# The squares of a norm added up on VectorE, with one ones-matmul for each norm instead of eight

## The chip, the cores and the metric

The kernel runs on one core of a Trainium2 chip. Five engines work side by side and signal each other by semaphores: TensorE (PE, matrix products from SBUF into PSUM banks), VectorE (DVE), ScalarE (ACT), GpSimd (POOL) and SyncE (SP), which issues the loads of weights. The metric is the time of one launch on the device in microseconds (us).

## The reference, cut to what matters

The program computes two model parts one after the other on 256 tokens of 1024 numbers, in float32. The first part has two layers; 16 meta tokens stand ahead of the sequence, so it works on 272 tokens:

```python
def rmsnorm(x, g):
    y = x32 * lax.rsqrt(jnp.mean(x32 * x32, axis=-1, keepdims=True) + NORM_EPS)
    return (y * g.astype(jnp.float32)).astype(x.dtype)

for l in range(DEPTH):                                   # DEPTH = 2
    hn = rmsnorm(h, norm1_g[l])
    proj = hn @ w_in[l]                                  # q, k, v and the convolution's input
    ...                                                  # rotary embedding
    attn_out = diff_attention(q, k, v, lam, subln_g[l], lam_init)
    conv_out = conformer_conv(u + b_glu[l], ...)         # gated, causal, layer norm, swish
    h = h + jnp.concatenate([attn_out, conv_out], axis=-1) @ w_out[l]
    hn = rmsnorm(h, norm2_g[l])
    gate, up = jnp.split(hn @ w_gate_up[l], 2, axis=-1)
    h = h + (jax.nn.silu(gate) * up) @ w_down[l]
h = rmsnorm(h, final_g)
```

The second part normalises the result again (its gain is g_mix), scales and shifts it by numbers that a small matrix w_ada yields, runs a gated delta rule and a dilated attention on it (the mixer), and then a mixture of 64 experts with eight chosen for a token.

A norm needs one number for each token: the mean over 1024 channels of the squares. That is a sum across the partitions of SBUF and over eight tiles, and it is what the change is about.

## The kernel before, in words

Activations lie transposed: 128 channels on the partitions, tokens along a row, eight tiles (KC = 8) for the 1024 channels; h[:, k] is tile k, 272 (T) or 256 (S) columns wide. In layer 1 everything after the attention is computed for the 256 real tokens only.

**Weights and products.** `weights` loads a block of 1024 x 256 weights by SP into `raw`, casts it on ACT into `hi` (f32r, a float32 form that PE reads at its fast rate; two halves, L165) and computes the rest `lo` on DVE (L166, two halves). There are three slots each for raw, hi and lo; a cast into a slot waits until PE has finished with the block that was in it. `mm3` does each product in three f32r matmuls: hi by xh (L172), hi by xl (L173), lo by xh (L174), where xh + xl is the activation. `block2` takes two PSUM banks and runs all eight k for both. The pool `mm` has three PSUM banks: with gate banks pg[0] and pg[1] and the first up bank pu[0] taken, pu[1] waits for one of them to be evicted.

**The norm.** `norm_in` (L262 to L280) does not normalise its input. It casts h times the gain into xh (L270, ACT) and xl (L271, DVE), and the products run on these. Beside them it squares each tile on ACT (L275) and multiplies it by a matrix of ones on PE (L276, plain float32), eight times into one bank of the pool `ax`, so that every partition holds the sum of squares of each token. `rsqrt` then takes the square root on ACT (L201, out of the bank, with a table load ahead of it) and the reciprocal on DVE (L202): rstd. Only the evictions of the products multiply by rstd: L361 and L362 for w_in (the a and gate halves of the convolution's input), L589 and L590 for the gate and up halves of the FFN. So an mm bank can't be emptied before rstd is there.

`norm_in` is called four times: norm 1 of layer 0, norm 2 of layer 0, norm 1 of layer 1 (272 columns each) and norm 2 of layer 1 (256 columns). While the last FFN's w_down runs, `mix_tile` does the same for the two norms that meet there, the final one and the mixer's: per tile two squares (L662, one with final_g as its scale) and two ones-matmuls (L663), into two `ax` banks that `mix_begin` takes. `mixer` reads the first in L692 (m), the second in L695, and computes from them the factor with which the tiles hh and hl are made (L704, L705), which the mixer's first matmuls read.

**The order of the work.** Nothing is ordered by hand here. The program is written in sequence, and a scheduler with a simulated timeline decides the order of the instructions on each engine when the kernel is built; `high_priority(offset=...)` lets marked pieces move ahead (250 for weights and mix_tile, 200 for the squares, the ones-matmuls and rsqrt of a norm). On the chip each engine works through its list in that order. An instruction that is priced or placed differently can so change the order of others near it. At the end of layer 1's attention the scheduler interleaves the attention's last norm (L465 squares of the head outputs, L201 and L202 on `oss`, L468, L470, the transposes L474 on PE, and L477 and L478, which write the attention half of w_out's input `bigb`) with the convolution's channel norm (L512 to L515, L201 and L202 on `sd`, L519, the tanh L521, L522, L524, L526, L527, which write the other half).

Of the kernel before, what the change touches and what calls it, by code (L numbers as in the profile page):

```python
# [9 lines left out]
F32 = mybir.dt.float32  # L10
# [3 lines left out]
OP = mybir.AluOpType  # L14

NM, S, D = 16, 256, 1024
T = NM + S
QT = ((0, 16), (16, 128), (144, 128))
KC = D // 128
# [90 lines left out]
class K:  # L110
# [151 lines left out]
    def norm_in(s, h, g, t0, n):  # L262

        ap, A, V = s.ap, s.A, s.V
        xh = ap.tile([128, KC, T], F32R, name="xh")
        xl = ap.tile([128, KC, T], F32R, name="xl")
        ss = s.ax()
        sl = slice(t0, t0 + n)
        for k in range(KC):
            A.activation(xh[:, k, sl], h[:, k, sl], AF.Copy, scale=g[:, k:k + 1])  # L270
            V.scalar_tensor_tensor(xl[:, k, sl], h[:, k, sl], g[:, k:k + 1], xh[:, k, sl].bitcast(F32),  # L271
                                   op0=OP.mult, op1=OP.subtract)
            sq = ap.tile([128, T], F32, name="sq", bufs=3)
            with s.tc.high_priority(offset=200):
                A.activation(sq[:, :n], h[:, k, sl], AF.Square)  # L275
                s.PE.matmul(ss[:, :n], s.C["ones"], sq[:, :n], start=(k == 0), stop=(k == KC - 1))  # L276
        r = ap.tile([128, T], F32, name="rstd", bufs=2)
        with s.tc.high_priority(offset=200):
            s.rsqrt(r[:, sl], ss[:, :n], s.eps5, 1.0 / D)
        return (xh, xl), r  # L280

# [368 lines left out]
    def mix_begin(s):  # L650
        P, V, cp = s.P2, s.V, s.cp
        s.gm = cp.tile([128, KC], F32, name="gm")
        V.scalar_tensor_tensor(s.gm, s.mod[:, 1], 1.0, P["g_mix_2"], op0=OP.add, op1=OP.mult)
        V.tensor_tensor(s.gm, s.gm, P["final_g"], op=OP.mult)
        s.msum = (s.ax(), s.ax())

    def mix_tile(s, h, hg, k):

        A, PE, hs = s.A, s.PE, slice(NM, T)
        for p, g in zip(s.msum, (1.0, s.P2["final_g"][:, k:k + 1])):  # L660
            a = s.ap.tile([128, S], F32, name="nsq", **s.nsq)
            A.activation(a, h[:, k, hs], AF.Square, scale=g)  # L662
            PE.matmul(p[:, :S], s.C["ones"], a, start=(k == 0), stop=(k == KC - 1))  # L663
        A.activation(hg[:, k, hs], h[:, k, hs], AF.Copy, scale=s.gm[:, k:k + 1])

    def mixer(s):
# [1027 lines left out]
```

## Time and profile before

| | |
|---|---|
| median of 3 runs | 1671.23 us (1670.63 to 1674.64) |
| the profiled execution | 1669.04 us |
| its span, first to last instruction | 1667.2 us, mean granted clock 0.984 |
| busy: PE, DVE, ACT | 1598.1 us (96%), 865.5 us (52%), 744.5 us (45%) |
| PE MATMUL records of L276 and L663 | 64 and 32 |
| HBM, last 500 us | some 420 GB/s |

The span is that of the profiled execution, which is one run of its own; 1.8 us of its time lie outside the span. Busy shares of different engines overlap. The records of PE's matmuls overlap among themselves as well: each is longer than the distance to the next one's start, so time on PE is read from starts. The expert weights, 64 loads each of three matrices, are what moves in the last 500 us.

### The profile page before, as it was taken

The page shows a single profiled execution, that of the slowest core. Times are in us where ns is not written, and L with a number is a line of the kernel's source. Part 1 is how long each engine was busy: PE and PEld are TensorE (multiplying, and loading weights), DVE is VectorE, ACT ScalarE, POOL GpSimd, SP SyncE. Part 2 cuts the span into 40 slices and gives each one's busy share as a digit, 9 for nine tenths or more (in the row PEclk, how much of TensorE's full clock was granted, in tenths as well). Part 3 has the DMA queues.
Part 4 walks back from the last instruction along what each step waited for, and adds up shares of the span by engine and source line. Part 5 has one row for each costly group of instructions (what it writes and reads, how often), then busy time and mean ns, then how long its engine had stood idle before and what let it go on. Part 6 is the DMA issues. An engine that isn't in the chain of part 4 may idle for free.

```text
span 1667.2 us, 32866 instructions
## 1 busy us (share of the span) xinstructions
PE 1598.1 (96%) x13630; PEld 1358.0 (81%) x13630; DVE 865.5 (52%) x1764; ACT 744.5 (45%) x1492; POOL 14.4 (1%) x28
## 2 busy tenths in 40 slices
PE   7999999999999999989999999999899999999897
PEld 6966999999968999988999999999666576566463
DVE  6685766646987666458656654553422221222122
ACT  5376644445347544455856856643322211112121
POOL 2000000000000000000000000000000000000000
PEclk9999999999999999999999999999899999999999
DMA  8408655555466555754343342666799999999995
GB/s 249 140 26 274 194 179 174 172 172 174 130 203 192 176 189 171 234 167 140 114 128 102 102 129 89 233 191 223 285 365 421 420 419 420 420 420 420 420 420 243
DMA packets 209959, 389.29 MB, mean 234 GB/s; under 512 B 8855, under 2 KB 183313, under 8 KB 184977
## 3 DMA queue, kind: packets, MB, share of 16 engines
q1 hardware_dynamic: 209104, 386.66, 64.0%
q8 instruction: 108, 1.77, 0.5%
q0 software_dynamic: 704, 0.51, 0.3%
q14 instruction: 43, 0.34, 0.1%
HBM read 386.10 MB, written 1.05 MB: 232 GB/s over the span
## 4 chain that ended last, share of the span: by engine, by line
PE 76%; DMA 14%; ACT 5%; DVE 4%; issue 1%; SPq 0%; DVEq 0%; ACTq 0%
PE mm L172 14%; PE mm L173 14%; PE mm L174 14%; PE pm L1508 6%; DMA we<-in_w_exp_up 6%; PE pm L1534 4%; DMA we<-in_w_exp_down 3%; DMA we<-in_w_exp_gate 2%; PE pm L1472 2%; PE dx L488 2%; PE mm L195 2%; PE mm L196 1%; PE mm L197 1%; ACT hi L165 1%; DMA raw<-in_w_out 1%; PE dx L630 1%
## 5 line engine op out<-in xcount | busy, mean ns | idle before, releaser
L166 DVE TENSOR_TENSOR lo<-raw,hi 128x1024 fp32r<-128x1024 f32 (+2 forms) x300 | 347.9, 1192 | 144.2 <-ACT hi L165 142.9
L165 ACT CAST hi<-raw 128x1024 fp32r<-128x1024 f32 (+2 forms) x300 | 292.7, 1024 | 271.0 <-PE mm L173 150.5
L172 PE MATMUL mm<-xh,hi 128*128 128x272 f32 (+1 forms) x1008 | 288.1, 288 | 0.0
L173 PE MATMUL mm<-xl,hi 128*128 128x272 f32 (+1 forms) x1008 | 287.8, 286 | 0.0
L174 PE MATMUL mm<-xh,lo 128*128 128x272 f32 (+1 forms) x1008 | 286.6, 286 | 0.0
L1508 PE MATMUL pm<-we,xT 128*32 128x256 f32 (+2 forms) x2048 | 195.9, 392 | 8.4 <-DMA we<-in_w_exp_up 5.8
L173 PEld LDWEIGHTS mm<-xl,hi 128*128 128x128 f32 x1008 | 189.7, 188 | 0.9
L174 PEld LDWEIGHTS mm<-xh,lo 128*128 128x128 f32 x1008 | 189.4, 188 | 0.5
L172 PEld LDWEIGHTS mm<-xh,hi 128*128 128x128 f32 x1008 | 188.5, 188 | 0.7
L1508 PEld LDWEIGHTS pm<-we,xT 128*32 128x32 f32 (+2 forms) x2048 | 122.2, 129 | 76.0 <-DMA we<-in_w_exp_up 7.9
L173 PE MATMUL mm<-bigb,hi 128*128 128x256 f32 (+1 forms) x512 | 148.3, 290 | 0.1
L172 PE MATMUL mm<-hh,hi 128*128 128x256 f32 x384 | 110.6, 291 | 7.2 <-ACT hh L704 4.2
L1534 PE MATMUL pm<-we,hT 128*32 128x512 f32 (+2 forms) x512 | 112.5, 605 | 0.1
L173 PE MATMUL mm<-hl,hi 128*128 128x256 f32 x384 | 109.5, 286 | 0.7 <-DVE hl L705 0.7
L174 PE MATMUL mm<-hh,lo 128*128 128x256 f32 x384 | 108.4, 285 | 0.0
L1519 DVE SCALAR_TENSOR_TENSOR hp<-sil,cs,pm 128x256 f32<-128x256 f32 x26 | 17.6, 676 | 168.5 <-ACT sil L1517 168.5
L174 PE MATMUL mm<-biga,lo 128*128 128x272 f32 (+1 forms) x352 | 101.4, 288 | 0.0
L172 PE MATMUL mm<-biga,hi 128*128 128x272 f32 (+1 forms) x352 | 100.6, 286 | 0.0
L173 PEld LDWEIGHTS mm<-bigb,hi 128*128 128x128 f32 x512 | 97.5, 191 | 0.8 <-DVE bigb L478 0.3
L1539 DVE TENSOR_TENSOR y<-pm,gt 128x512 f32<-128x512 f32 x52 | 35.9, 689 | 119.5 <-PE pm L1534 119.5
L1517 ACT ACTIVATE sil<-pm 128x256 f32<-128x256 f32 x26 | 10.0, 384 | 175.2 <-PE pm L1508 175.2
L195 PE MATMUL mm<-hi,hh 128*128 128x256 f32 x288 | 85.8, 298 | 2.0 <-DVE cacc L861 2.0
(541 smaller groups left out, 3089.7 us busy)
## 6 DMA issues: line engine op xcount, KB each, us to landing
we<-in_w_exp_gate SPq DMA_DIRECT2D x64, 1024.0 KB, 19.6
we<-in_w_exp_up SPq DMA_DIRECT2D x64, 1024.0 KB, 19.8
we<-in_w_exp_down SPq DMA_DIRECT2D x64, 1024.0 KB, 19.7
raw<-in_w_in SPq DMA_DIRECT2D x62, 1024.0 KB, 5.3
raw<-in_w_gate_up SPq DMA_DIRECT2D x44, 1024.0 KB, 5.1
raw<-in_w_ada SPq DMA_DIRECT2D x22, 1024.0 KB, 6.0
raw<-in_w_down SPq DMA_DIRECT2D x16, 1024.0 KB, 5.1
raw<-in_w_out SPq DMA_DIRECT2D x12, 1024.0 KB, 6.7
```

What stands on the lines that cost most here:

```text
L165: s.A.copy(hi[:, a:b], raw[:, a:b])
L166: s.V.tensor_tensor(lo[:, a:b], raw[:, a:b], hi[:, a:b].bitcast(F32), op=OP.subtract)
L172: s.PE.matmul(ps[:, :n], a, xh, start=start, stop=False)
L173: s.PE.matmul(ps[:, :n], a, xl, start=False, stop=False)
L174: s.PE.matmul(ps[:, :n], b, xh, start=False, stop=stop)
L195: s.PE.matmul(p[:, :256], xh, w[0][:, k], start=(k == 0), stop=False)
L488: PE.matmul(p[:, :nq], dg, z[:, c, tq + j:tq + j + nq], start=(j == 0), stop=(j == n - 1))
L1472: s.PE.matmul(p[:, 256 * kk:256 * kk + 256], s.ht[h][:, i, k + kk], oh[:, i], start=(i == 0 and h == 0), stop=(i == 1 and h == 1))
L1508: mm = PE.matmul(gu[sg, 256 * m:256 * m + 256], xT[:, k, o + sg.start:o + sg.stop], w[m][:, k], start=(k == 0), stop=(k == 7))
L1519: V.scalar_tensor_tensor(hp.rearrange("p k q -> p q k"), sil.rearrange("p (q k) -> p q k", k=2), cs, gu[:, 256:].rearrange("p (q k) -> p q ...
L1534: PE.matmul(py[sg], hT[:, k, sg], w[2][:, k, 512 * j:512 * j + 512], start=(k == 0), stop=(k == 1))
L1539: V.tensor_tensor(y, py, s.gt2[:, 512 * j:512 * j + 512], op=OP.mult)
```

## The change

In `norm_in` the square of tile 0 is written into a tile `sqsum`, and DVE adds the other seven squares to it (L278 of the changed file). After the loop one ones-matmul (L282) sums `sqsum` over the partitions into the `ax` bank, which is taken only then, and rsqrt follows as before. In `mix_tile` two tiles msq0 and msq1 collect the squares (L668), and at the last tile the two banks are taken and two ones-matmuls issued (L672). The pool tiles borrow the places of tiles that exist already (tags sd and vf). Counted in the code, 32 + 16 ones-matmuls become 4 + 2, and 28 + 14 additions come in.

```diff
--- before.py
+++ after.py
@@ -264,18 +264,22 @@
         ap, A, V = s.ap, s.A, s.V
         xh = ap.tile([128, KC, T], F32R, name="xh")
         xl = ap.tile([128, KC, T], F32R, name="xl")
-        ss = s.ax()
         sl = slice(t0, t0 + n)
+        tot = ap.tile([128, T], F32, name="sqsum", tag="sd")
         for k in range(KC):
             A.activation(xh[:, k, sl], h[:, k, sl], AF.Copy, scale=g[:, k:k + 1])
             V.scalar_tensor_tensor(xl[:, k, sl], h[:, k, sl], g[:, k:k + 1], xh[:, k, sl].bitcast(F32),
                                    op0=OP.mult, op1=OP.subtract)
-            sq = ap.tile([128, T], F32, name="sq", bufs=3)
+
+            sq = ap.tile([128, T], F32, name="sq", bufs=3) if k else tot
             with s.tc.high_priority(offset=200):
                 A.activation(sq[:, :n], h[:, k, sl], AF.Square)
-                s.PE.matmul(ss[:, :n], s.C["ones"], sq[:, :n], start=(k == 0), stop=(k == KC - 1))
+                if k:
+                    V.tensor_tensor(tot[:, :n], tot[:, :n], sq[:, :n], op=OP.add)
         r = ap.tile([128, T], F32, name="rstd", bufs=2)
         with s.tc.high_priority(offset=200):
+            ss = s.ax()
+            s.PE.matmul(ss[:, :n], s.C["ones"], tot[:, :n], start=True, stop=True)
             s.rsqrt(r[:, sl], ss[:, :n], s.eps5, 1.0 / D)
         return (xh, xl), r
 
@@ -652,15 +656,20 @@
         s.gm = cp.tile([128, KC], F32, name="gm")
         V.scalar_tensor_tensor(s.gm, s.mod[:, 1], 1.0, P["g_mix_2"], op0=OP.add, op1=OP.mult)
         V.tensor_tensor(s.gm, s.gm, P["final_g"], op=OP.mult)
-        s.msum = (s.ax(), s.ax())
+        s.msq = [s.ap.tile([128, S], F32, name=f"msq{i}", tag=("sd", "vf")[i], bufs=1 + i) for i in range(2)]
 
     def mix_tile(s, h, hg, k):
 
         A, PE, hs = s.A, s.PE, slice(NM, T)
-        for p, g in zip(s.msum, (1.0, s.P2["final_g"][:, k:k + 1])):
-            a = s.ap.tile([128, S], F32, name="nsq", **s.nsq)
+        for t, g in zip(s.msq, (1.0, s.P2["final_g"][:, k:k + 1])):
+            a = s.ap.tile([128, S], F32, name="nsq", **s.nsq) if k else t
             A.activation(a, h[:, k, hs], AF.Square, scale=g)
-            PE.matmul(p[:, :S], s.C["ones"], a, start=(k == 0), stop=(k == KC - 1))
+            if k:
+                s.V.tensor_tensor(t, t, a, op=OP.add)
+        if k == KC - 1:
+            s.msum = (s.ax(), s.ax())
+            for p, t in zip(s.msum, s.msq):
+                PE.matmul(p[:, :S], s.C["ones"], t, start=True, stop=True)
         A.activation(hg[:, k, hs], h[:, k, hs], AF.Copy, scale=s.gm[:, k:k + 1])
 
     def mixer(s):
```

Behind `norm_in` the lines of the changed file are 4 higher, behind `mix_tile` 9: L589 becomes L593, L361 L365, L477 L481, L521 L525.

The scheduler's order moves in three places. In the rows below the number behind a name tells one buffer from another; a wait names the engine whose signal the instruction stands for.

First, norm 2 of layer 0, on ACT. hi_2142 is the fourth weight block of the FFN, rstd the factor. Before:

```order
L165 CAST hi_2134<-raw_2132 128x1024
L275 ACTIVATE sq_1992<-h_1743 128x272 [waits DVE_49,Activation_49]
L270 ACTIVATE xh_1952<-h_1743,pc_norm2_g_747 128x272
L201 ACT_TABLE_LOAD
L201 ACTIVATE rstd_1995<-ax_1954,eps5_75 128x272 [waits PE_49]
L165 CAST hi_2142<-raw_2140 128x1024 [waits DMAHW6_49,PE_49]
L165 CAST hi_2142<-raw_2140 128x1024
```

and now:

```order
L270 ACTIVATE xh_1952<-h_1743,pc_norm2_g_747 128x272
L276 ACTIVATE sq_1990<-h_1743 128x272 [waits DVE_49,Activation_49]
L270 ACTIVATE xh_1952<-h_1743,pc_norm2_g_747 128x272
L165 CAST hi_2142<-raw_2140 128x1024 [waits DMAHW6_49,PE_49]
L165 CAST hi_2142<-raw_2140 128x1024
L201 ACT_TABLE_LOAD
L201 ACTIVATE rstd_1993<-ax_1994,eps5_75 128x272 [waits PE_49]
```

The cast of hi_2142, which waits for PE to release a slot, stands ahead of the table load and the square root; before it stood behind them. Norm 2 of layer 1 shows the same exchange.

At the same place on PE (mm_2016 and mm_2017 are the gate banks of the first block, mm_2066 and mm_2067 its up banks). Before:

```order
L173 MATMUL mm_2017<-xl_1953,hi_2002 128x272
L276 MATMUL ax_1954<-sq_1992,blob0_73 128x272 [waits Activation_49]
L174 MATMUL mm_2017<-xh_1952,lo_2003 128x272
L172 MATMUL mm_2016<-xh_1952,hi_2002 128x272
L173 MATMUL mm_2016<-xl_1953,hi_2002 128x272 [waits DVE_49]
L174 MATMUL mm_2016<-xh_1952,lo_2003 128x272
L172 MATMUL mm_2017<-xh_1952,hi_2002 128x272
L173 MATMUL mm_2017<-xl_1953,hi_2002 128x272
```

and now:

```order
L174 MATMUL mm_2016<-xh_1952,lo_2003 128x272
L173 MATMUL mm_2017<-xl_1953,hi_2002 128x272
L174 MATMUL mm_2017<-xh_1952,lo_2003 128x272
L173 MATMUL mm_2066<-xl_1953,hi_2010 128x272
L282 MATMUL ax_1994<-sqsum_1954,blob0_73 128x272 [waits DVE_49]
L174 MATMUL mm_2066<-xh_1952,lo_2011 128x272
L172 MATMUL mm_2067<-xh_1952,hi_2010 128x272 [waits DVE_49]
L173 MATMUL mm_2067<-xl_1953,hi_2010 128x272
L174 MATMUL mm_2067<-xh_1952,lo_2011 128x272
```

Before, the last ones-matmul stood 38 places ahead of the first matmul into mm_2067; now the only one stands two places ahead of it, behind the last matmul that reads the first block's hi and lo (mm_2017 of lo_2003).

Second, norm 1 of layer 1, on DVE, where a1 and g1 are evictions of the a and gate halves. Before:

```order
L271 SCALAR_TENSOR_TENSOR xl_4094<-h_3452,pc_norm1_g_92,xh_4093 128x272 [waits DVE_49,Activation_49] x2
L202 RECIPROCAL rstd_4136<-rstd_4136 128x272 [waits Activation_49]
L361 TENSOR_TENSOR a1_4258<-mm_4158,rstd_4136 128x272 [waits DVE_49,PE_49]
L361 TENSOR_TENSOR a1_4265<-mm_4159,rstd_4136 128x272 [waits PE_49]
L369 TENSOR_TENSOR biga_4139<-blob1_181,rstd_4136 128x272
L370 TENSOR_TENSOR biga_4139<-blob1_181,rstd_4136 128x272
```

and now:

```order
L278 TENSOR_TENSOR sqsum_4095<-sqsum_4095,sq_4131 128x272 [waits DVE_49]
L202 RECIPROCAL rstd_4134<-rstd_4134 128x272 [waits Activation_49]
L166 TENSOR_TENSOR lo_4283<-raw_4280,hi_4282 128x1024 [waits DMAHW0_49,PE_49,Activation_49]
L166 TENSOR_TENSOR lo_4283<-raw_4280,hi_4282 128x1024 [waits Activation_49]
L365 TENSOR_TENSOR a1_4258<-mm_4158,rstd_4134 128x272 [waits DVE_49]
L366 TENSOR_TENSOR g1_4259<-mm_4208,rstd_4134 128x272 [waits PE_49]
L365 TENSOR_TENSOR a1_4265<-mm_4159,rstd_4134 128x272
```

The two halves of lo_4283 have come between the reciprocal and the first eviction. On ACT the square root stays ahead of the cast here, and on PE the ones-matmul stands ten places ahead of the first matmul into mm_4209.

Third, the end of layer 1's attention, on ACT. Before:

```order
L465 ACTIVATE scr_5034,oss_5015<-mm_5014,st_4749 128x128 [waits Activation_49]
L201 ACTIVATE oss_5015<-oss_5015,eps5_75 128x4 [waits Activation_49]
L201 ACTIVATE sd_5372<-ax_5371,eps5_75 128x256 [waits PE_49]
L477 ACTIVATE bigb_4140<-mm_5041,subg_749 128x4x128 [waits PE_49]
L521 ACT_TABLE_LOAD
L521 ACTIVATE sq_5393<-biga_4139,hlb_751,hlg_750 128x256 [waits DVE_49]
L521 ACTIVATE sq_5400<-biga_4139,hlb_751,hlg_750 128x256 [waits DVE_49]
L522 ACTIVATE biga_4139<-biga_4139,pc_norm2_g_747 128x256 [waits Activation_49]
L521 ACTIVATE sq_5407<-biga_4139,hlb_751,hlg_750 128x256 [waits DVE_49]
```

and now:

```order
L469 ACTIVATE scr_5034,oss_5015<-mm_5014,st_4749 128x128 [waits Activation_49]
L201 ACTIVATE sd_5372<-ax_5371,eps5_75 128x256 [waits PE_49]
L201 ACTIVATE oss_5015<-oss_5015,eps5_75 128x4 [waits Activation_49]
L525 ACT_TABLE_LOAD
L525 ACTIVATE sq_5393<-biga_4139,hlb_751,hlg_750 128x256 [waits DVE_49]
L525 ACTIVATE sq_5400<-biga_4139,hlb_751,hlg_750 128x256 [waits DVE_49]
L526 ACTIVATE biga_4139<-biga_4139,pc_norm2_g_747 128x256 [waits Activation_49]
L525 ACTIVATE sq_5407<-biga_4139,hlb_751,hlg_750 128x256 [waits DVE_49]
L526 ACTIVATE biga_4139<-biga_4139,pc_norm2_g_747 128x256 [waits Activation_49] x2
L530 ACTIVATE bigb_4140<-biga_4139 128x256 [waits DVE_49]
L525 ACTIVATE sq_5414<-biga_4139,hlb_751,hlg_750 128x256
L481 ACTIVATE bigb_4140<-mm_5041,subg_749 128x4x128 [waits PE_49]
```

L477 (now L481), which writes the attention half of w_out's input, followed the square roots; now the table load and eight instructions of the channel norm stand between.

## Rows read from the trace of the kernel before

**Rows 1.** The page: the chain that ended last, by engine.
```profile
PE 76%; DMA 14%; ACT 5%; DVE 4%; issue 1%; SPq 0%; DVEq 0%; ACTq 0%
```

**Rows 2.** By line: the ones-matmuls (count, ns min/median/max, first and last start).
```profile
L276 PE MATMUL ax<-sq,blob x64: 377/391/661, 18.3 to 546.9; 128*128 128x272 f32 x48, 128*128 128x256 f32 x16
...
L663 PE MATMUL ax<-nsq,blob x32: 377/379/483, 687.8 to 740.8; 128*128 128x256 f32 x32
```

**Rows 3.** Timeline, PE, norm 2 of layer 0 (start us, us, instruction, idle before).
```profile
199.19 0.62 PE L276 MATMUL ax<-sq,blob 128*128 128x272 f32 x2
199.45 0.49 PE L174 MATMUL mm<-xh,lo 128*128 128x272 f32 x1
199.77 0.29 PE L172 MATMUL mm<-xh,hi 128*128 128x272 f32 x1
...
201.41 0.29 PE L173 MATMUL mm<-xl,hi 128*128 128x272 f32 x1
```

**Rows 4.** Timeline, PE, norm 2 of layer 1.
```profile
546.73 0.59 PE L276 MATMUL ax<-sq,blob 128*128 128x256 f32 x2
...
547.27 0.28 PE L174 MATMUL mm<-xh,lo 128*128 128x256 f32 x1
```

**Rows 5.** Timeline, PE, norm 1 of layer 0.
```profile
18.33 2.47 PE L276 MATMUL ax<-sq,blob 128*128 128x272 f32 x6
```

**Rows 6.** Timeline, PE, the end of the last FFN and the mixer's start.
```profile
737.86 1.81 PE L663 MATMUL ax<-nsq,blob 128*128 128x256 f32 x6 [0.42 <-ACT nsq L662]
...
740.53 0.68 PE L663 MATMUL ax<-nsq,blob 128*128 128x256 f32 x2
...
745.48 0.79 PE L172 MATMUL mm<-hh,hi 128*128 128x256 f32 x2 [4.18 <-ACT hh L704]
```

**Rows 7.** By line: an addition of two such tiles on DVE.
```profile
L592 DVE TENSOR_TENSOR a<-a,g x44: 415/428/442, 205.8 to 668.6; 128x272 f32<-128x272 f32 x22, 128x256 f32<-128x256 f32 x22
```

**Rows 8.** Timeline, ACT, norm 2 of layer 0.
```profile
199.85 0.49 ACT L201 ACTIVATE rstd<-ax,eps 128x272 f32<-128x272 f32 x1 [1.38 <-PE ax L276]
201.74 2.00 ACT L165 CAST hi<-raw 128x1024 fp32r<-128x1024 f32 x2 [1.40 <-PE mm L173]
```

**Rows 9.** Timeline, ACT, ahead of w_out in layer 1.
```profile
513.60 0.47 ACT L201 ACTIVATE sd<-ax,eps 128x256 f32<-128x256 f32 x1
515.37 0.69 ACT L477 ACTIVATE bigb<-mm,subg 128x512 fp32r<-128x512 f32 x1 [1.30 <-PE mm L474]
516.07 1.28 ACT L521 ACT_TABLE_LOAD   x1
...
520.65 0.59 ACT L521 ACTIVATE sq<-biga,hlb,hlg 128x256 f32<-128x256 f32 x1
```

**Rows 10.** Timeline, DVE, norm 2 of layer 0.
```profile
200.37 1.85 DVE L202 RECIPROCAL rstd<-rstd 128x272 f32<-128x272 f32 x1 [2.09 <-ACT rstd L201]
202.33 0.79 DVE L589 TENSOR_TENSOR g<-mm,rstd 128x272 f32<-128x272 f32 x2
203.03 2.35 DVE L166 TENSOR_TENSOR lo<-raw,hi 128x1024 fp32r<-128x1024 f32 x2
```

**Rows 11.** Timeline, PE, the first matmul of w_out in layer 1.
```profile
516.11 0.50 PE L172 MATMUL mm<-bigb,hi 128*128 128x256 f32 x2 [0.78 <-ACT bigb L477]
```

**Rows 12.** Timeline, DVE, ahead of w_out in layer 1.
```profile
513.93 0.69 DVE L470 TENSOR_TENSOR osb<-mm,oss 128x512 f32<-128x512 f32 x1
514.53 1.74 DVE L202 RECIPROCAL sd<-sd 128x256 f32<-128x256 f32 x1
...
516.76 1.42 DVE L519 TENSOR_TENSOR biga<-biga,sd 128x256 f32<-128x256 f32 x4
```

**Rows 13.** Timeline, ACT, the end of the last FFN.
```profile
740.15 0.46 ACT L692 ACTIVATE m<-ax,eps 128x256 f32<-128x256 f32 x1
```

**Rows 14.** Windows: busy us by engine, granted clock (PEclk), DMA share, GB/s.
```profile
510.00:520.00 10.00, 6.97 (x44) 5.43 (x44) 7.03 (x13) 8.53 (x23) 0.00 (x0) 1.00 0.61 202
...
743.80:750.60 6.80, 4.43 (x19) 4.14 (x20) 6.58 (x18) 3.79 (x10) 0.00 (x0) 0.50 0.26 71
```

## Prediction

> **What bounds the kernel now.** I read the chain of work that ended last first: TensorE (PE) carries 76% of it, and DMA 14%, the expert weights at the end [rows 1]. An instruction taken off PE's stream before the experts is therefore time won, and a wait put into it is time lost. Next came the lines of the ones-matmuls: 64 records of L276 and 32 of L663, two records to each f32 matmul in the code, so 32 and 16 matmuls [rows 2]. Then I read PE's timeline around them, because records of one engine overlap and their lengths can't be added.
>
> **What a ones-matmul costs.** At the second norm of layer 0 the pair starts at 199.19; one matmul stands behind it, and the next starts at 199.77: 0.58 us for the pair and one ordinary slot. Thirteen slots lie between 199.77 and 201.41, 0.126 us each [rows 3]. The pair takes 0.58 - 0.126 = 0.455 us of the stream. With 256 columns it is 546.73 to 547.27, 0.54 less a slot of 0.12, so 0.42 us [rows 4]. The lengths of the two records (0.391 each by [rows 2]) would give 0.78 us.
> The Trainium skill ("FP8 and Floating Point Precision", TensorE Precision Notes) says that true FP32 goes through the array in four passes. By that rule one such matmul is worth four slots, by estimate 4 x 0.126 = 0.50 us; the trace has 0.455, so starts and rule stand together against the summed records. By the records all 42 removed matmuls would be worth 32 us, by the starts 18.
>
> **What the change removes.** Four calls of norm_in and one series of mix_tile, in order of time:
> - A, norm 1 of layer 0: 8 matmuls become 1. Six records stand alone from 18.33 to 20.43 ahead of the first weight matmul [rows 5]: 2.1 us at most; the others, four net, 4 x 0.455 = 1.8.
> - B, norm 2 of layer 0, and C, norm 1 of layer 1: 7 x 0.455 = 3.2 us each.
> - D, norm 2 of layer 1 (256 columns): 7 x 0.42 = 2.9.
> - E, the two sums of mix_tile: 16 become 2. Four pairs (six records from 737.86, two at 740.53) run in PE's idle tail before the mixer and save nothing [rows 6]; 12 x 0.42 = 5.0.
> All of it: 3.9 + 3.2 + 3.2 + 2.9 + 5.0 = 18.2 us.
>
> **What it adds.** 28 + 14 additions on VectorE (DVE), 0.43 us each by the like operation L592 [rows 7]: 18 us, on an engine that the page shows busy for 52% of the span. That alone would be covered. What counts is where the sum becomes ready. Before, the last square's matmul runs as soon as the square is there; rstd is ready while PE still fills banks it owns. Now the single matmul waits for the last addition, and the order of the instructions shows it one matmul before PE needs a new bank at B and D, nine before it at C. That bank is freed by the first eviction (L589, L361 of before), and the eviction multiplies by rstd.
>
> **The new stall at B.** On ScalarE (ACT) the cast of the next weight (L165, two halves) has moved ahead of the square root. The cast waits for PE to give back a hi slot, which it does with the L173 started at 201.41; the cast follows at 201.74 [rows 3, 8], 0.33 us later. From there: cast to next 2.01 (2.00 and a hand-over), table load 1.28 [rows 9], square root 0.52 to the reciprocal's start, reciprocal 1.96 to L589, L589 0.44 and 0.05 to PE [rows 8, 10]. Sum 0.33 + 2.01 + 1.28 + 0.52 + 1.96 + 0.44 + 0.05 = 6.6 us. PE has, from that L173, four slots and the ones pair: 4 x 0.126 + 0.455 = 0.96. Stall 5.6, saving 3.2: B = +2.4. Before there was no such stall since square root (199.85) and reciprocal (200.37) preceded the cast [rows 8, 10].
> **D** has the same order with 256 columns: 6.4 - 0.9 = 5.5 of stall, less 2.9: +2.6.
> **C** keeps the square root ahead of the cast, but on DVE the two halves of lo (L166, 2.35 [rows 10]) come between reciprocal and eviction. From the ones matmul: 0.66 to the square root (199.19 to 199.85), 0.52, 1.96, 2.35, 0.44, 0.05 = 6.0; PE has the pair and nine slots, 0.455 + 1.13 = 1.6. Stall 4.4, less 3.2: +1.2.
> **A**: saving 3.9; but seven additions (3.0) stand among the lo casts with which PE's first matmuls begin, and rstd is late there too. Ends: -3.9 if all is kept, +1.7 with the 5.6 of B; I take 0, near the middle, since the additions alone return most of it.
> **The front of layer 1's w_out.** Other work is re-ordered too. L477, which lets PE start w_out at 516.11 [rows 11], now stands on ACT behind the table load and the convolution's L521/L522/L526 that followed it before. From that load (516.07) to the end of the last L521 (520.65, and 0.5 more to its successor) is 5.1 us; put behind the square roots, whose second ends at 513.60 + 0.47 = 514.07, L477 would start at 519.1 instead of 515.37 [rows 9]: +3.8. If ACT reaches its square roots up to 0.9 sooner (one L514 fewer ahead of them), +2.9. DVE agrees: L470 (513.93 before) comes behind both reciprocals and the four L519, 1.74 + 0.18 + 1.42 later [rows 12]. I take +3.5. The rest of layer 1's attention is re-ordered as well; nothing prices it, so 0, with +-3.
> **E**: the chain into the mixer now has an addition (0.43) and a ones matmul that starts only then (0.66 to its reader) where L692 read its bank at 740.15 [rows 13]: about +1.0 on a path that PE waits for (4.18 us before 745.48 [rows 6]). E = -5.0 + 1.0 = -4.0.
> Sum at full clock: 0 + 2.4 + 1.2 + 3.5 + 2.6 - 4.0 = +5.7 us.
>
> **The clock.** After the 4.18 us of idle PE ran at half clock, granted 0.50, the 1.2 GHz level, from 743.80 to 750.60 [rows 6, 14]. Work from 745.48 on took 5.1 us that would have taken half: 2.6 lost. The shorter gaps around w_out left it at 1.00 [rows 14]. Stalls of 5.6, 4.4 and 5.5 us are longer than the one that cost the clock, so I charge three times 2.5 = +7.5; the w_out front, whose idle time is broken by transposes, nothing (at most 2.6 more).
> **Sum.** +5.7 + 7.5 = +13.2. The profiled execution took 1669.04 us, 2.2 below the median of 1671.23; 1669.04 + 13.2 + 2.2 = 1684.4. Nothing later takes the delay back: the expert stream is fed through buffers that the mixer frees, so it starts later by as much.
>
> **Rivals.** Here 0.3%, 5 us, is what a measurement can tell from no change.
> 1. The stalls come, the clock stays: 1671.2 + 5.7 = 1677. For it: the 0.78 us gap at w_out [rows 11] cost no clock, and the stalls might be shorter than I sum. Against: 4.18 us did. Chance 0.25, of it a quarter within 5 us.
> 2. Savings and waits cancel, or the delay is hidden behind DMA: the last 500 us run at 420 GB/s, and if the expert loads don't start later the end stays: 1671. For it, DMA's 14%; against, 76% of PE ahead of it. Chance 0.12.
> 3. Faster: rstd is ready in time. Place: ACT's queue at B and D and DVE's at C. It decides where the ones matmul ends over 6 us before PE's third bank is full; then no stall, no lost clock, and only E's +1.0 and the w_out front stay against 18.2: 1671.2 - 18.2 + 1.0 + 3.5 = 1657; with w_out unhurt 1654. For it: before, PE's matmuls ran on without a gap here [rows 3, 4]. Against: the instruction order, one matmul ahead of the bank. Chance 0.13.
> Forecast: 0.50, own range 1679 to 1692 (two to four clock losses, +-3 for what is not priced).
> The range that leaves 2 in 10 out goes from 1671 to 1692: outside lie case 3, half of case 2 and a little above. Slower 0.50 + 0.19 = 0.69; within 0.06 + 0.12 = 0.18; faster 0.13.
>
> **What would show it.** Three waits of PE for an eviction (L593, L365 of the changed kernel) of 4 to 6 us, each with a half-clock stretch of some 5 us behind it; on ACT the cast before the square root; PE's w_out in layer 1 starting 3 to 4 us later after its attention; six ones matmuls and 42 additions of about 0.43. Wrong if PE shows no wait there over 2 us (then case 3), if those stretches stay at full clock (case 1), or if the mixer starts later by over 10 us and the end doesn't move (case 2).

## The result, and the profile after

The changed kernel takes 1681.79 us (median of 10 runs, 1679.32 to 1688.79) against 1670.39 us (10 runs, 1666.83 to 1674.64): ratio 1.0077, 95% interval 1.0061 to 1.0092. It is 11.4 us slower; 1684.4 was forecast. Its runs lie in two groups, 1679 to 1683 and 1687 to 1689, with mean granted clocks of 0.975 to 0.978 and 0.969 to 0.972; the first profiled execution (1688.79 us) is of the upper group, a second (run e5 below, 1679.18 us) of the lower. The three waits that matter below are the same in both, so the stages are read from the second.

What was removed and added is as the code says. By line, in the first trace of the changed kernel (records, ns min/median/max, first and last start):

```profile
L282 PE MATMUL ax<-sqsum,blob x8: 377/390/467, 33.0 to 567.7; 128*128 128x272 f32 x6, 128*128 128x256 f32 x2
...
L672 PE MATMUL ax<-msq,blob x4: 634/634/636, 760.2 to 761.5; 128*128 128x256 f32 x4
...
L278 DVE TENSOR_TENSOR sqsum<-sqsum,sq x28: 415/431/436, 17.3 to 563.7; 128x272 f32<-128x272 f32 x21, 128x256 f32<-128x256 f32 x7
...
L668 DVE TENSOR_TENSOR msq<-msq,nsq x14: 414/420/427, 711.4 to 760.1; 128x256 f32<-128x256 f32 x14
```

Twelve records, six matmuls, stand where 96 records stood [rows 2], and 42 additions of 0.42 to 0.43 us are new, as priced from [rows 7]. Three of the things PE waited for, over the whole of the second trace (us in total, times, longest):

```profile
PE mm L172 <- DVE g L593: 10.7, 2, 5.4
...
PE mm L478 <- DVE osb L474: 5.0, 1, 5.0
...
PE mm L172 <- DVE a L365: 4.7, 2, 3.9
```

The first trace has the same three lines, 10.7, 5.0 and 4.7. Before, no wait of PE for such an eviction stands in the list. The two waits for L593 and the longer one for L365 are the forecast ones: 5.4, 5.4 and 3.9 us. The timeline at norm 2 of layer 0 shows how one comes about; ACT, DVE and PE (start us, us, instruction, idle before it):

```profile
201.38 1.99 ACT L165 CAST hi<-raw 128x1024 fp32r<-128x1024 f32 x2 [5.29 <-PE mm L173]
203.39 1.28 ACT L201 ACT_TABLE_LOAD   x1
204.68 0.49 ACT L201 ACTIVATE rstd<-ax,eps 128x272 f32<-128x272 f32 x1
```
```profile
205.20 1.85 DVE L202 RECIPROCAL rstd<-rstd 128x272 f32<-128x272 f32 x1 [0.38 <-ACT rstd L201]
207.09 0.44 DVE L593 TENSOR_TENSOR g<-mm,rstd 128x272 f32<-128x272 f32 x1
```
```profile
201.31 0.29 PE L173 MATMUL mm<-xl,hi 128*128 128x272 f32 x1
201.43 0.62 PE L282 MATMUL ax<-sqsum,blob 128*128 128x272 f32 x2
201.69 0.49 PE L174 MATMUL mm<-xh,lo 128*128 128x272 f32 x1
207.59 0.59 PE L172 MATMUL mm<-xh,hi 128*128 128x272 f32 x1 [5.41 <-DVE g L593]
207.98 0.43 PE L173 MATMUL mm<-xl,hi 128*128 128x272 f32 x1
208.20 0.43 PE L174 MATMUL mm<-xh,lo 128*128 128x272 f32 x1
```

PE issues the one ones-matmul at 201.43 and one product after it, and then has no bank. ACT holds the cast of the next weight first (201.38 to 203.37), then the table load, then the square root, the order that was [rows 8] the other way round. The reciprocal ends at 207.05, the first eviction begins at 207.09, PE goes on at 207.59. From there its starts lie 0.22 us apart and not 0.126: half clock. The windows give the clock (seventh number; the first pair is PE's busy time and records):

```profile
204.50:211.30 6.80, 3.71 (x16) 3.71 (x17) 4.10 (x7) 3.13 (x6) 0.00 (x0) 0.50 0.47 154
...
412.70:416.10 3.40, 3.40 (x17) 3.40 (x17) 1.13 (x3) 2.08 (x3) 0.00 (x0) 0.50 0.95 302
...
521.90:532.10 10.20, 6.69 (x30) 6.30 (x31) 5.54 (x15) 5.95 (x13) 0.00 (x0) 0.50 0.18 61
...
566.30:569.70 3.40, 3.34 (x15) 3.35 (x16) 1.42 (x5) 1.15 (x3) 0.00 (x0) 0.50 0.58 202
```

All four new waits are followed by a stretch at 1.2 GHz: three at the norms and one at w_out.

The stages, by the start of one marked instruction in each trace, in us and as the difference to before:

| at the start of | before | changed (1679.18 us) |
|---|---|---|
| first L574 of layer 0 (norm 1 and attention done) | 177.3 | +2.2 |
| last L574 of layer 0 (squares of norm 2 in the stream) | 194.6 | -1.0 |
| last L589 of layer 0 (wait for rstd behind it) | 321.6 | +5.0 |
| last L602 of layer 0 (squares of norm 1, layer 1) | 396.4 | +2.3 |
| last L361 of layer 1 (wait behind it) | 415.7 | +7.6 |
| first L574 of layer 1 (attention and w_out's front) | 525.5 | +12.3 |
| last L574 of layer 1 | 542.1 | +10.0 |
| last L589 of layer 1 (wait behind it) | 662.3 | +16.6 |
| last L602 of layer 1 (squares of mix_tile) | 735.6 | +11.3 |
| first L704 (mixer starts) | 744.9 | +12.4 |
| first L744 (end of the mixer's products) | 1016.4 | +14.6 |
| first L1508 (experts) | 1189.3 | +11.7 |
| last L1534 | 1654.2 | +10.1 |

The three norms from norm 2 of layer 0 on show the same two steps: 2.3 to 3.2 us saved while the squares pass, and more than that lost at the evictions.

These marks are mostly instructions of VectorE. On PE the same product can be compared, counted by its L172, before and in e5: in layer 0's w_out it starts at 178.82 and 179.75 (+0.9); in the FFN behind the first wait at 216.32 and 221.37 (+5.0); at norm 1 of layer 1 just ahead of the wait at 405.77 and 407.61 (+1.8), behind it at 415.15 and 422.71 (+7.6); in layer 1's w_out at 526.50 and 539.06 (+12.6); behind the last wait at 561.98 and 578.59 (+16.6). So the first mark, +2.2, is 1.3 more than PE lost.

### The profile page after: what moved, and what is told of

It reads as the page before. It is cut to its first block, busy times and chain, and to the rows that moved or that the text cites. A ratio compares the mean times of both kernels' runs of the same rounds, so it can differ in the third digit from the quotient of the medians.

```text
span 1687.0 us, 32747 instructions
## 1 busy us (share of the span) xinstructions
PE 1594.0 (94%) x13546; PEld 1355.3 (80%) x13546; DVE 878.9 (52%) x1806; ACT 745.1 (44%) x1492; POOL 14.5 (1%) x28
## 4 chain that ended last, share of the span: by engine, by line
PE 78%; DMA 9%; ACT 5%; DVE 5%; SPq 1%; issue 1%; ACTq 0%; DVEq 0%
PE mm L172 14%; PE mm L173 14%; PE mm L174 14%; PE pm L1517 8%; PE pm L1543 4%; DMA we<-in_w_exp_up 4%; DMA we<-in_w_exp_down 3%; PE pm L1481 2%; PE dx L492 2%; PE mm L195 2%; PE mm L196 1%; PE mm L197 1%; ACT hi L165 1%; PE dx L634 1%; DMA we<-in_w_exp_gate 1%; DMA raw<-in_w_out 1%
## 5 line engine op out<-in xcount | busy, mean ns | idle before, releaser
L172 PE MATMUL mm<-xh,hi 128*128 128x272 f32 (+1 forms) x1008 | 290.2, 291 | 15.4 <-DVE g L593 10.7
L173 PE MATMUL mm<-xl,hi 128*128 128x272 f32 (+1 forms) x1008 | 291.2, 290 | 0.6 <-DVE xl L271 0.6
L174 PE MATMUL mm<-xh,lo 128*128 128x272 f32 (+1 forms) x1008 | 290.5, 289 | 0.9 <-DVE lo L166 0.9
L172 PEld LDWEIGHTS mm<-xh,hi 128*128 128x128 f32 x1008 | 191.5, 191 | 17.2 <-DVE g L593 11.4
L173 PEld LDWEIGHTS mm<-xl,hi 128*128 128x128 f32 x1008 | 193.1, 192 | 1.5 <-DVE xl L271 0.8
L172 PE MATMUL mm<-hh,hi 128*128 128x256 f32 x384 | 111.0, 292 | 7.1 <-ACT hh L713 4.4
L172 PE MATMUL mm<-biga,hi 128*128 128x272 f32 (+1 forms) x352 | 100.1, 284 | 0.0
```

The lines of the kernel that those rows point to most:

```text
L172: s.PE.matmul(ps[:, :n], a, xh, start=start, stop=False)
L173: s.PE.matmul(ps[:, :n], a, xl, start=False, stop=False)
L174: s.PE.matmul(ps[:, :n], b, xh, start=False, stop=stop)
```

## The experiments

My theory, **1**: PE waits for a bank whose eviction waits for a late rstd; the front of layer 1's w_out is re-ordered; clock is lost behind the waits. Rival **2**: the additions burden VectorE and everything that it feeds.

**Each half alone** (e1: norm_in changed, mix_tile as before; e2: the other way round).

> The change in norm_in alone; mix_tile as before. Theory 1 (late factor: PE waits for evictions that wait for rstd, the re-ordered front of w_out, and lost clock): the whole change's 1681.8 us without the 4.0 us that the mixer's part gains, so about 1685.8, with waits of 4 to 5.5 us for the first eviction at three norms. Theory 2 (the additions themselves burden VectorE): 28 of the 42 additions, two thirds of the loss of 11.4, so about 1678.

> The change in mix_tile alone; norm_in as before. Theory 1: twelve ones-matmuls off a dense PE stream, 5.0 us, less 1.0 us on the chain into the mixer: 1670.4 - 4.0 = 1666.4. Theory 2: 14 of the 42 additions cost a third of 11.4: 1674.

Measured: e1 1689.92 us (ratio 1.0115, 1.0097 to 1.0132), e2 1674.91 (1.0031, 1.0015 to 1.0046). The waits in e1 are the forecast ones: its three lines of that kind are those of the changed kernel to the tenth (10.7, 5.0 and 4.7 us).

e1 is 4 us above what theory 1 gave. Against e5 its trace loses 1.4 us more up to the end of layer 0's attention, 1.6 more in layer 1's and 1.5 more in the mixer; the cause of the first two is open. e2 went against it outright: slower, where 4 us were to be won, and just the 1674 of theory 2.

**The last square sent to PE directly** (e3), and **additions that nobody reads** (e4):

```diff
 # cut to the lines that count
 # e3, in norm_in; mix_tile likewise
+                if k == KC - 1:
+                    ss = s.ax()
+                    s.PE.matmul(ss[:, :n], s.C["ones"], tot[:, :n], start=True, stop=False)
+                    s.PE.matmul(ss[:, :n], s.C["ones"], sq[:, :n], start=False, stop=True)
+                elif k:
                     V.tensor_tensor(tot[:, :n], tot[:, :n], sq[:, :n], op=OP.add)
 # e4, in the kernel before, ahead of the ones-matmul, which stays
+                if k:
+                    V.tensor_tensor(tot[:, :n], sq[:, :n], sq[:, :n], op=OP.add)
```

> Squares 0 to 6 are added on VectorE, the last one goes to PE directly, so two ones-matmuls for each sum and no addition behind the last square. The built order has the square root ahead of the cast again, 15, 20 and 15 PE slots between the last ones-matmul and the awaited bank, and layer 1's w_out front as before. Theory 1: from ones-matmul to evicted bank 0.66 + 0.52 + 1.96 + 1.22 (half a lo) + 0.44 + 0.05 = 4.85 us against 2.3 to 2.9 us of PE work: waits of about 2 to 2.5 us at three norms, savings of 2.7 each, 5.0 in the mixer's part: 1663 to 1667 us. Theory 2: 36 of 42 additions: about 1680.

> The kernel before with 28 additions on VectorE in norm_in whose result nobody reads; all eight ones-matmuls stay. Theory 1: additions on a VectorE that has time cost 0 to 2 us: 1670 to 1673. Theory 2: the additions alone cost what the change lost plus what it saved, (11.4 + 18.2) x 28/42 = 20 us: 1690; a weaker form of it, half of their 12 us of busy time, 1676.

Measured: e3 1679.51 us (1.0062, 1.0042 to 1.0081), e4 1682.31 (1.0066, 1.0049 to 1.0083). Both totals speak for theory 2 again. The traces do not. In e3 the waits at the norms shrank as theory 1 had worked out:

```profile
PE mm L172 <- DVE g L595: 4.2, 2, 2.1
...
PE mm L172 <- DVE a L367: 2.2, 2, 1.4
```

(2.1 us twice, and 1.4.) And the stages before the mixer came out near what theory 1 gave: the mixer started 4.4 us earlier in e2 (4.0 expected), 2.8 earlier in e3 (3.4 or more expected), 0.9 later in e4 (0 to 2). The loss lies behind that start, in the mixer, which none of these edits touches. First starts of hh and of zs, the mixer's first and one of its last activations, before, in e2 and in e4:

```profile
L704 ACT ACTIVATE hh<-nt,mod x8: 492/494/513, 744.9 to 749.8; 128x256 fp32r<-128x256 f32 x8
...
L744 ACT ACTIVATE zs<-mm x8: 378/385/406, 1016.4 to 1051.5; 128x256 f32<-128x256 f32 x8
```
```profile
L709 ACT ACTIVATE hh<-nt,mod x8: 492/495/510, 740.5 to 745.4; 128x256 fp32r<-128x256 f32 x8
...
L749 ACT ACTIVATE zs<-mm x8: 376/385/406, 1021.4 to 1056.5; 128x256 f32<-128x256 f32 x8
```
```profile
L708 ACT ACTIVATE hh<-nt,mod x8: 492/494/510, 745.8 to 750.7; 128x256 fp32r<-128x256 f32 x8
...
L748 ACT ACTIVATE zs<-mm x8: 376/385/406, 1034.8 to 1070.0; 128x256 f32<-128x256 f32 x8
```

From 744.9 to 1016.4 are 271.5 us, in e2 280.9 and in e4 289.0. The windows over that stretch, before and e4, hold the same work, 3254 and 3259 records of PE:

```profile
745.00:1016.00 271.00, 259.09 (x3254) 249.15 (x3255) 171.42 (x345) 180.97 (x421) 2.76 (x2) 0.98 0.38 118
```
```profile
745.00:1035.00 290.00, 268.56 (x3259) 258.59 (x3260) 172.43 (x347) 186.92 (x426) 2.75 (x2) 0.95 0.36 111
```

PE is busy for 259 and 269 us of them and idle for 12 and 21. So about half of the longer time is waiting, and half is the same work taking longer at a mean granted clock of 0.95 instead of 0.98. (The traced execution of e4, 1686.85 us, is the slowest of six, 4.5 above their median, so some of the 289.0 belongs to that execution.) PE's waits in the mixer of e4 that are longer than before (there 1.2, 0 and 0.6 us):

```profile
PE mm L172 <- DVE cacc L865: 3.6, 2, 3.2
PE ax L955 <- DVE bigb L939: 2.7, 3, 2.1
PE ax L872 <- ACT nsq L870: 2.5, 1, 2.5
```

The traces show the order in which the mixer's instructions ran. From the first hh to the first zs, with repeats taken as one, before has 1672 rows on PE and 354 on ACT. Of these 87 and 38 stand elsewhere in e2, 87 and 39 in e3, 147 and 58 in e4, 72 and 23 in e1; in the changed kernel 4 and 2. So **theory 3**: the scheduler orders the mixer by its simulated time, and an edit far ahead that shifts it can re-order the mixer, at a price that has nothing to do with the edit.

**The same kinds of edit with the mixer's order kept** (e6, e7, e8; e5 is the changed kernel again). Among kernels that send the last one to five squares directly, those were chosen whose built order of the mixer is that of before.

```diff
 # e6 and e8, in mix_tile: squares 0 to 4 added, 5 to 7 directly
+            if k >= 5:
+                if k == 5:
+                    s.msum.append(s.ax())
+                    PE.matmul(s.msum[-1][:, :S], s.C["ones"], t, start=True, stop=False)
+                PE.matmul(s.msum[0 if t is s.msq[0] else 1][:, :S], s.C["ones"], a, start=False, stop=k == KC - 1)
+            elif k:
                 s.V.tensor_tensor(t, t, a, op=OP.add)
 # e8, in norm_in: squares 0 to 5 added, 6 and 7 directly, in the same way
 # e7: as e4, with k from 0
```

> The changed kernel once more, for a second trace. Theory 1: the three waits of 5.4, 3.9 and 5.4 us are in the instruction order and come again to a tenth; what differs from the first trace (1688.8 us, 7 above the median) is clock alone: fewer half-clock stretches around layer 1's attention than the 30 us of the first, and a mixer start at some 759 to 763 us instead of 766. If the waits differ, theory 1 is wrong about their cause.

> norm_in as before; in mix_tile the squares 0 to 4 are added (8 additions) and 5 to 7 go to PE directly (4 ones-matmuls for each sum instead of 8). The built order of the mixer is the one of the kernel before, but for a handful of rows. Theory 3 (the loss of the mixer-only run arose in the mixer, from its new instruction order): the mixer starts some 3.4 us earlier (8 matmuls of 0.42) and takes as long as before: 1667 us. Theory 2 (additions cost, 0.3 to 0.6 us each): -3.4 + 2.4 to 4.8: 1669 to 1672.

> As the run with 28 unread additions, with 32 (tile 0 too); all eight ones-matmuls stay. The built order of the mixer is nearly that of the kernel before. Theory 3: with the mixer's order back, 32 additions cost the 1 us that the front of the 28 showed: 1670 to 1673, and the mixer takes 271 us from L861 to its end stage as before and not 289. Theory 2: 32/28 of the 11.9 us: 1684.

> In norm_in squares 0 to 5 are added and 6 and 7 go to PE directly (3 ones-matmuls); in mix_tile as in the run with five. The built order has the square root ahead of the cast at all norms, 28 to 30 slots of PE between the last ones-matmul and the awaited bank (37, 28 and 35 before), layer 1's w_out front and the mixer as before. Theories 1 and 3: no wait over 1 us for rstd, savings 2 x 2.3 + 2.1 + 3.4 = 10.1, up to 2 at norm 1 of layer 0: 1658 to 1662 us, faster than the kernel before. Theory 2: 28 additions cost 12 against 10: 1672.

Measured (the kernel before gave 1668.84 beside these, 23 runs): e5 1679.18 us (one run), e6 1665.98 (0.9974, 0.9958 to 0.9989), e7 1666.66 (0.9978, 0.9964 to 0.9992), e8 1656.49 (0.9921, 0.9899 to 0.9943). From the first hh to the first zs:

| | us | mixer starts |
|---|---|---|
| before | 271.5 | 744.9 |
| changed, e5 | 273.6 | +12.4 |
| e1 | 275.2 | +20.4 |
| e2 | 280.9 | -4.4 |
| e3 | 283.9 | -2.8 |
| e4 | 289.0 | +0.9 |
| e6 | 271.6 | -4.1 |
| e7 | 272.6 | +1.4 |
| e8 | 272.9 | -10.8 |

The pair for e7, to be held against that of e4:

```profile
L708 ACT ACTIVATE hh<-nt,mod x8: 493/496/509, 746.3 to 751.2; 128x256 fp32r<-128x256 f32 x8
...
L748 ACT ACTIVATE zs<-mm x8: 379/386/401, 1018.9 to 1054.1; 128x256 f32<-128x256 f32 x8
```

In e6, e7 and e8 the mixer's order is that of before but for at most 8 rows on PE and 3 on ACT. Thirty-two unread additions cost nothing that can be measured, where 28 had cost 12 us: theory 2 falls. Theory 3 fits all nine kernels: where the mixer's order is that of before, it takes 271.6 to 273.6 us; where it is not (e1 to e4), 275.2 to 289.0. That it is the scheduler's simulated time that moves the order is argued, not shown. That e7 came out 0.2% below the kernel before, where 1670 to 1673 was expected, stays unexplained: its trace is of the slowest of its twelve executions (1669.57 us) and can't show it. e5 had the three waits again; its mixer started at 757.4, a little ahead of the 759 to 763 expected. What it had less of is half clock around layer 1's attention: 13.6 us (504.8 to 508.2 and 521.9 to 532.1), against 30.7 in the first trace of the changed kernel:

```profile
490.70:511.20 20.50, 20.50 (x110) 11.65 (x109) 10.13 (x36) 9.50 (x31) 0.00 (x0) 0.50 0.61 192
528.30:538.50 10.20, 5.20 (x23) 4.80 (x24) 7.04 (x17) 6.79 (x14) 0.00 (x0) 0.50 0.31 104
```

PE worked for 25.7 of the 30.7 and for 10.1 of the 13.6 us. Half of the difference is 7.8 us; by the marks 7.2 of the 9.6 us between the two executions arise there. Why one execution had more half clock than the other is open. e8, at 1656.49 a little below the 1658 to 1662 expected, has, at its norms, the square root back ahead of the cast and no wait of PE for an eviction; norm 2 of layer 0 on ACT and DVE:

```profile
198.23 0.49 ACT L201 ACTIVATE rstd<-ax,eps 128x272 f32<-128x272 f32 x1 [1.98 <-PE ax L281]
200.49 2.01 ACT L165 CAST hi<-raw 128x1024 fp32r<-128x1024 f32 x2 [1.77 <-PE mm L173]
```
```profile
198.75 1.85 DVE L202 RECIPROCAL rstd<-rstd 128x272 f32<-128x272 f32 x1 [3.00 <-ACT rstd L201]
200.70 0.79 DVE L596 TENSOR_TENSOR g<-mm,rstd 128x272 f32<-128x272 f32 x2
```

The eviction (L596) starts 1.6 us earlier than L589 did at 202.33 [rows 10]. e8 beats both kernels: 12 us below the kernel before beside it, 25 below the change.

**A fourth bank** (e9, e10): `mm` with four banks and `ax` with two, in the kernel before and in the changed one.

> The kernel before with four PSUM banks for products (mm) and two instead of three for ax. A control for the next run: fewer ax banks hold up the attention, so slower than before by some 15 to 30 us. With eight ones-matmuls PE never waited for rstd, so the fourth bank brings nothing at the norms under any theory.

> The changed kernel with the same four mm and two ax banks. Theory 1 (PE waits for a bank that only an eviction with rstd frees): with a fourth bank 25 to 33 slots (3 to 4 us) lie between the ones-matmul and the awaited bank instead of 1 to 9, the square root stands ahead of the cast, no wait for an eviction over 2 us at the norms, and the same change now gains 6 to 12 us against its control. Theory 4 (the loss comes from elsewhere: the additions, the front of w_out, the order of norm 1 of layer 0): it loses or stays within 5 us of its control.

Measured: e9 1710.62 us (1705.03 to 1713.38), e10 1694.45 (1691.63 to 1698.01); the kernel before gave 1672.52 beside them. The control lost more than expected, 38 us. The same change that lost 11.4 us with three banks gains 16.2 with four, somewhat more than the 6 to 12 expected. In e10:

```profile
PE mm L172 <- DVE g L593: 1.8, 2, 1.0
...
PE mm L172 <- DVE a L365: 0.9, 1, 0.9
```

The longest wait for an eviction is 1.0 us instead of 5.4, and the mixer starts 13.0 us ahead of e9's; the mixers of the two run in the same order but for two rows. On ACT the square root of norm 2 of layer 0 stands ahead of the cast:

```profile
209.00 0.49 ACT L201 ACTIVATE rstd<-ax,eps 128x272 f32<-128x272 f32 x1 [5.14 <-PE ax L282]
209.38 1.99 ACT L165 CAST hi<-raw 128x1024 fp32r<-128x1024 f32 x2
```

So the loss at the norms is the awaited bank. The bank and the order on ACT changed together, and no run separates them. Theory 4 falls for the additions, which e10 has too, and for norm 1 of layer 0, behind which e10 stands 0.5 us ahead of e9 (first L574 of layer 0). It does not fall for the front of w_out: e9 and e10 wait there alike (their lines in turn), so the pair says nothing of its share.

```profile
PE mm L474 <- DVE osb L470: 15.4, 2, 8.1
...
PE mm L478 <- DVE osb L474: 15.7, 2, 8.1
```

## Why the prediction was right

By its own steps, from e5 and in us (A to D and w_out by PE's products, the rest by the marks):

| step | forecast | measured |
|---|---|---|
| A | 0 | +0.9 |
| B: saved, then waited | -3.2, 5.6 | -3.2, 5.4 |
| C: saved, then waited | -3.2, 4.4 | -3.2, 3.9 |
| w_out's front with layer 1's attention | +3.5 | +5.0, of it some 3 clock |
| D: saved, then waited | -2.9, 5.5 | -3.0, 5.4 |
| E: saved, then later m | -5.0, +1.0 | -5.3, +1.1 |
| clock behind the three waits | +7.5 | 5.2 |
| up to the mixer's start | +13.2 | +12.4 |
| mixer, experts | 0 | +2.2, -4.5 |

The savings of B and D are what is left when wait and clock are taken off the growth of PE's delay (B: 4.1 - 5.4 - 1.9; D: 4.0 - 5.4 - 1.7); C's is read just ahead of its wait.

**What held.** The three waits and their place in the order, the savings, E, and the half clock behind each wait. A pair of ones-matmuls was worth its starts (0.455 us) and not its records (0.78, which would make 5.5 of B's 3.2). The chain from released slot to freed bank gave 5.6 and 5.5; the waits were 5.4. With the square root ahead of the cast again and more of the sum on PE, the waits fell to 2.1 (e3) and to none (e8). At w_out the reason was the forecast one:

```profile
523.74 1.11 PE L478 MATMUL mm<-blob,osb 128*128 128x128 f32 x4 [4.98 <-DVE osb L474]
526.52 0.79 PE L172 MATMUL mm<-bigb,hi 128*128 128x256 f32 x2 [1.67 <-ACT bigb L481]
```
```profile
525.80 0.66 ACT L481 ACTIVATE bigb<-mm,subg 128x512 fp32r<-128x512 f32 x1
```

L481 starts at 525.80 instead of 515.37, 10.4 later, 7.6 of which came in with it; 2.8 against +3.5 forecast. Rivals 1 and 2 fall with the same rows: all three waits have their half clock, and of the mixer's +12.4 us 9.9 are left at the end of the span.

A lay within its bounds of -3.9 and +1.7. Behind norm 1's products PE is 2.3 us late, but 1.4 of that it had at its first matmul (before, then e5):

```profile
PE ax L214 <- DMA pv_norm_g<-in_b_glu: 11.7, 1, 11.7
...
PE ax L214 <- DMA pv_norm_g<-in_b_glu: 13.1, 1, 13.1
```

In every other trace that first load also came later than in the one of before (12.6 to 14.1). e2 and e6, whose norm_in is untouched, are 2.3 and 2.2 late at the same product. From PE's first matmul to its first weight product it takes 6.5 us instead of 8.7, so the early start was worth 2.2, as priced (2.1). What took that back are waits for rstd (0.8), lo (0.9) and two shorter ones, 2.2 in all, and products that follow each other at larger distances, whose cause is open.

**What was mis-sized.** The clock: PE worked at half clock from 207.59 to 211.3, 412.7 to 416.1 and 566.3 to 569.7, 3.4 to 3.7 us each and not 5, 10.5 us together, half of which is 5.2 lost, not 7.5; and the w_out front, charged nothing, had 6.7 us of it. C's wait was 3.9 and not 4.4. A and w_out were too low by 0.9 and 1.5. These errors partly cancel, and so do the mixer and the experts, which were put at 0: that the total came within 3 us of the forecast is in part luck. "Nothing later takes the delay back" was wrong in detail: of the 14.6 us at the mixer's end 10.1 are left at the end of the experts. A part is clock, granted 0.82 and 0.91 in the 37 us around the start of the experts, before and in e5:

```profile
1167.80:1204.80 37.00, 30.11 (x190) 22.93 (x192) 16.06 (x66) 12.44 (x23) 0.00 (x0) 0.82 0.66 270
```
```profile
1182.40:1219.40 37.00, 31.46 (x220) 23.52 (x222) 19.54 (x76) 14.07 (x26) 0.00 (x0) 0.91 0.74 306
```

The rest stays open.

**What the prediction did not see.** It took work that the edit doesn't touch for unmoved, but for w_out. That the changed kernel's mixer kept its order (+2.2 us) was luck of this edit; half of the same edit lost 9.4 us there (e2), the other half 3.7 (e1). Rival 3 asked for rstd in time; e8 shows it is to be had, by sending the last squares to PE directly.

## What to carry to other kernels

An operation taken off the bound engine brings time only if the result that its successor waits for does not come later: a sum that was spread over eight steps ends one step after its last input, while one gathered elsewhere adds a whole chain behind it. Price the first consumer that is short of a buffer, here a bank, and leave the last steps of the sum as they were. How many was chosen here by the mixer's order too: e3 does the same with one square and lost 9 us to another order. Where a scheduler orders the program, compare the order of stages the edit doesn't touch before blaming the edit, and read experiments stage by stage: three totals here (e2, e3, e4) pointed at the wrong theory.

## What the runs showed of the hardware that was not expected

The changed kernel had half clock (granted 0.50) around layer 1's attention for 30.7 us in one trace and for 13.6 in the other, with the same three waits; the whole took 1688.79 us at a mean granted clock of 0.972 and 1679.18 at 0.979. A wait of 3.9 us (C) was followed by 3.4 us at 1.2 GHz. At w_out 10.2 us followed waits of 5.0 and 1.7, where the prediction had charged nothing since the front's gaps before had left the clock alone [rows 14]. In e3 two waits of nearly the same length differ: 3.4 us at half clock (206.5 to 209.9) follow the one of 2.0 us at norm 2 of layer 0, while the one of 2.1 us at norm 2 of layer 1 is followed by full clock.
